# A hybrid encoder block on one core: the softmax of attention in a stage of its own, behind the next slot's turned queries

## The chip, the cores and the metric

The kernel runs on one core of a Trainium2 chip. The metric is the device time of one execution in microseconds (us); several executions are timed and their median is compared. One further execution is recorded by the profiler, and all rows below come from it.

## The reference, cut to what matters

One encoder block on a sequence of 1024 tokens with 1024 features, in float32. Two branches read the same normalised and projected input: gated linear attention, and windowed attention with grouped queries (8 query heads, 2 key and value heads of 128 features, blocks of 128 queries that see three blocks of 128 keys). The branches are merged, and a gated feed-forward layer follows. The change touches the windowed attention alone:

```python
q = _rope(_rms_norm(q...), pos); k = _rope(_rms_norm(k...), pos)
...
scores = jnp.einsum("bnqhgd,bnkhd->bnhgqk", qb, kc) * (hd ** -0.5)
scores = jnp.where(mask[None, :, None, None], scores, -jnp.inf)
sink = sinks.astype(f32).reshape(1, 1, hkv, grp, 1, 1)
m = jnp.maximum(scores.max(axis=-1, keepdims=True), sink)
p = jnp.exp(scores - m)
denom = p.sum(axis=-1, keepdims=True) + jnp.exp(sink - m)
o = jnp.einsum("bnhgqk,bnkhd->bnqhgd", p / denom, vc)
```

## The kernel before

Every float32 matrix product is made of three passes on TensorE (the engine PE): each operand is split into a high and a low part (`wh` and `wl`, `xh` and `xl`, `sqh` and `sql`, `ph` and `pl`), and high times high, low times high and high times low are summed in PSUM. The high part is a copy on ScalarE (ACT), the low part a subtraction on VectorE (DVE). So each operand costs one instruction on either engine.

The stage of windowed attention runs from about 390 to 570 us. Its work is cut into 16 units, one for each pair of a query block t and a key head g (four query heads each). A unit passes through a pipeline of six slots of the loop over `todo`; its steps and lines are:

- `prep` (L690 to 716, once for a block): load the projected queries and the next block's keys and values, squares (L696, L702), their sums (L704, on DVE), inverse roots, `rope_k`.
- `a_rope` (L725 to 728): the rotary products on DVE (L674, L676, L677).
- `a_turn` (L730 to 740): TensorE transposes the four heads of queries; ACT copies them out as `sqh` (L737), DVE makes `sql` (L738). `k_turn` does the same for keys (L721, L722).
- `a_scores`, four calls, one a head (L742 to 772): three score passes (L73), then a DVE instruction that adds the band mask and takes the row maximum (L752, the row-max). The last call also does the softmax of all four heads: on DVE the scaled maximum `mx` (L759), its bound by the sink `nm` (L760), `es` (L762); on ACT the exponentials (L763 for the sink, L766 four times, which also sum the row); on DVE the denominator `dn` (L768) and its reciprocal `rd` (L770); on ACT the normalising multiplication (L772, four times).
- `a_probs`, three calls, one a key block (L774 to 788): transposes of the probabilities, `ph` (L786) and `pl` (L787).
- `a_out` (L790 to 800): nine passes into one output, a copy `st` (L797) and its stores.

Unit n turns its queries in slot n+2, makes its scores in slot n+3, its probabilities' transposes in slot n+4 and its output in slot n+5. In one slot the steps of different units stand in the order `prep, a_rope, a_scores, a_turn, k_turn, a_out, a_probs`. So the softmax of a unit, written in the fourth call of `a_scores`, stands ahead of the turn of the following unit. Between two steps `slot` calls `fill`, which issues matrix products of the dense projections of the same input (L73 and L246 with the tile `mm`): TensorE has these while a step waits for the other engines.

TensorE's order is written out by hand (`tc.manual_schedule(engines={PE})`). The order on ACT, DVE and the DMA queue of SyncE (SP) comes from a scheduler that takes the program's order as its priority and places an instruction when it reckons its operands ready; `with tc.issue_after(x)` adds the one condition that what is written inside stands behind x on its engine. PSUM has four banks for dense products (`mm`) and four for the rest (`ch`). A new `ch` tile takes the bank that comes free first in the scheduler's order, and TensorE waits for the last reader of that bank.

Of the kernel before, what the change touches and what calls it, by code (L numbers as in the profile page):

```python
# [11 lines left out]
AF = mybir.ActivationFunctionType  # L12
# [12 lines left out]
SF = ((2, 50), (9, 24), (18, 18), (1 << 30, 12))  # L25
# [5 lines left out]
def body(tc, i, out):  # L31
    nc = tc.nc
    with ExitStack() as root:
# [8 lines left out]
        def nm(s):  # L42
            uid[0] += 1
            return f"{s}_{uid[0]}"
# [4 lines left out]
        def chtile(shape, dt=F32):  # L49
            return psc.tile(list(shape), dt, tag="ch", name=nm("ch"))  # L50
# [24 lines left out]
        def mm3(o, ah, al, bh, bl, start, stop):  # L75
            mm(o, ah, bh, start, False)
            mm(o, ah, bl, False, False)
            mm(o, al, bh, False, stop)
# [179 lines left out]
        def fill(n):  # L258

            while n > 0 and dense:  # L260
                try:
                    next(dense[0])
                    n -= 1
                except StopIteration:
                    dense.pop(0)

        def share(plan, t):
            return next(n for end, n in plan if t < end)
# [5 lines left out]
        def slot(stages, n):  # L274

            stages = [f for f in stages if f]
            done = 0
            if not stages:
                fill(n)
            for j, f in enumerate(stages):  # L280
                f()
                t = n * (j + 1) // len(stages)
                fill(t - done)
                done = t
# [340 lines left out]
        with tc.manual_schedule(engines={mybir.EngineType.PE}):  # L625
            fill(36)
            for t in range(last + 1):
                work = [[at[t, j]] for j in (0, 5, 4, 3, 2, 1) if (t, j) in at]
                if t in behind:
                    work = work or [[]]  # L630
# [38 lines left out]
        keys, att = {}, {}  # L669
# [60 lines left out]
        def a_turn(g, n):  # L730
            a = att[g, n]
            qt = chtile((P, 4, P))
            for h in range(4):
                nc.tensor.transpose(qt[:, h], a.qn[:, h], ident)
            a.qh = sw.tile([P, 4, P], FR, tag="qh", name=nm("sqh"))
            a.ql = sw.tile([P, 4, P], FR, tag="ql", name=nm("sql"))
            nc.scalar.activation(a.qh, qt, AF.Copy)  # L737
            nc.vector.tensor_tensor(a.ql, qt, a.qh.bitcast(F32), op=ALU.subtract)  # L738
            a.b0, a.b1 = max(n - 1, 0), min(n + 1, KT - 1)
            a.w = (a.b1 - a.b0 + 1) * P  # L740

        def a_scores(g, n, h):  # L742
            a = att[g, n]
            if h == 0:
                a.p = sw.tile([P, 4, 384], F32, tag="p", name=nm("p"))
                a.mx = sw.tile([P, 4], F32, tag="mx", name=nm("mx"))
            w, p, mx = a.w, a.p, a.mx
            ks = slice(a.b0 * P, (a.b1 + 1) * P)
            mo = (a.b0 - (n - 1)) * P
            s = chtile((P, 384))  # L750
            mm3(s[:, :w], a.qh[:, h], a.ql[:, h], kTh[:, g, ks], kTl[:, g, ks], True, True)
            nc.vector.tensor_tensor_reduce(out=p[:, h, :w], in0=s[:, :w], in1=band[:, mo:mo + w],  # L752
                                           op0=ALU.add, op1=ALU.max, scale=1.0, scalar=-1e30,
                                           accum_out=mx[:, h:h + 1])
            if h < 3:
                return
            sk = sink[:, 4 * g:4 * g + 4]
            nm_ = sw.tile([P, 4], F32, tag="nm", name=nm("nm"))
            nc.vector.scalar_tensor_tensor(mx, mx, -1.0, a.rs, op0=ALU.mult, op1=ALU.mult)  # L759
            nc.vector.tensor_tensor(nm_, mx, nsink[:, 4 * g:4 * g + 4], op=ALU.min)  # L760
            es = sw.tile([P, 4], F32, tag="es", name=nm("es"))
            nc.vector.tensor_tensor(es, sk, nm_, op=ALU.add)  # L762
            nc.scalar.activation(es, es, AF.Exp)  # L763
            dn = sw.tile([P, 4], F32, tag="dn", name=nm("dn"))
            for h in range(4):
                nc.scalar.activation(p[:, h, :w], p[:, h, :w], AF.Exp, bias=nm_[:, h:h + 1],  # L766
                                     scale=a.rs[:, h:h + 1], accum_out=dn[:, h:h + 1])
            nc.vector.tensor_tensor(dn, dn, es, op=ALU.add)  # L768
            rd = sw.tile([P, 4], F32, tag="rd", name=nm("rd"))
            nc.vector.reciprocal(rd, dn)  # L770
            for h in range(4):
                nc.scalar.activation(p[:, h, :w], p[:, h, :w], AF.Copy, scale=rd[:, h:h + 1])  # L772
# [40 lines left out]
        def xpart(q, k):  # L813
            r = xn.tile([P, HT], F32, tag="xn", name=nm("xn"))
            nc.sync.dma_start(out=r, in_=scr[f"x{q}", k])
            pool, th, tl, d = homes[q]
            XT[q].append(xsplit(pool, th.format(k + d), tl.format(k + d), r))
# [4 lines left out]
        for n in range(2 * KT):  # L822
            t, g = divmod(n, 2)
            todo[n + 5].append((a_out, g, t))
            todo[n + 4] += [(a_probs, g, t, kb) for kb in range(3)]
            todo[n + 3] += [(a_scores, g, t, h) for h in range(4)]
            todo[n + 2].append((a_turn, g, t))
            todo[n + 1].append((a_rope, g, t))
            if g == 0:
                todo[n + 1].append((prep, t))  # L830
                if t + 1 < KT:
                    todo[n + 2].append((k_turn, t + 1))
        order = (prep, a_rope, a_scores, a_turn, k_turn, a_out, a_probs)
        with tc.manual_schedule(engines={mybir.EngineType.PE}):
            for t, v in enumerate(todo):
                v.sort(key=lambda e: order.index(e[0]))
                if t > 2 * KT + 2 and v:
                    fill(8)
                slot([lambda e=e: e[0](*e[1:]) for e in v], share(SF, t))
                if t >= 2 * KT + 2:  # L840
                    assert len(dense) == 1
                    for q in ("T1", "22"):
                        xpart(q, t - 2 * KT - 2)
# [81 lines left out]
        def pair_T3(f):  # L925
            nme, m, a, b = PAIRS[f]
            g = pend[f]
            product(g.X, wsplit(g.s3, 512), XT["T3"], 4, False, True)
            return result((f"{nme}{m + 4}", 1), g.X, g.p5)
# [69 lines left out]
        with tc.manual_schedule(engines={mybir.EngineType.PE}):  # L999
# [15 lines left out]
            for j in range(0, len(PAIRS), 2):  # L1015
# [4 lines left out]
                v = [pair_T3(f) for f in two]  # L1020
# [53 lines left out]
        def gate(nme, s):  # L1074
            g = bt.tile([P, HT], F32, tag=nme[:2], name=nm(nme[:2]))
            nc.sync.dma_start(out=g, in_=scr[nme, s])
            nc.scalar.activation(g, g, AF.Sigmoid)
            return g
# [119 lines left out]
        with tc.manual_schedule(engines={mybir.EngineType.PE}):  # L1198
# [29 lines left out]
            for m in (0, 4, 1, 5, 2, 6, 3, 7):  # L1228
                g = [gate(f"gb{m}", s) for s in range(2)]
# [352 lines left out]
```

## Time and profile before

| | |
|---|---|
| median of 3 runs | 1625.35 us (1625.33 to 1625.67) |
| the profiled execution | 1624.31 us, span of its instructions 1622.5 us |
| TensorE (PE) busy | 1611.6 us, 99% |
| VectorE (DVE) busy | 1223.9 us, 75% |
| ScalarE (ACT) busy | 915.0 us, 56% |
| granted TensorE clock | 1.00 |

A row of the list of instructions has the start (us from the span's start), the length, the engine, the line, the operation, output and inputs by name, and shapes; in brackets stands how long the engine was idle just ahead of it and what ended that. Matmuls are pipelined, so the distance from one start to the next is what a matmul costs and its length is more than that.

### The profile page before, as it was taken

How to read it: one execution, taken by the hardware profiler on the slowest of the kernel's cores; microseconds unless marked ns; L12 is line 12 of the kernel's file. 1: busy time of each engine (PE TensorE's matmuls, PEld its weight loads, DVE VectorE, ACT ScalarE, POOL GpSimd, SP SyncE). 2: the span in 40 equal slices, each digit the busy share in tenths (PEclk: the TensorE clock that was granted, in tenths of full speed). 3: DMA queues.
4: the chain of work that ended last, by engine and by line, in shares of the span. 5: the costliest groups of instructions: out<-in, count | busy, mean ns of one | idle time of the engine just before them, and what ended most of it. 6: DMA issues, size and time to landing. Idle time of an engine off the chain costs nothing.

```text
span 1622.5 us, 23392 instructions
## 1 busy us (share of the span) xinstructions
PE 1611.6 (99%) x7644; PEld 1341.5 (83%) x7644; DVE 1223.9 (75%) x2315; ACT 915.0 (56%) x1883; POOL 0.2 (0%) x4
## 2 busy tenths in 40 slices
PE   9999999999999999999999999999999999999999
PEld 7888888888888888888888888888888888888887
DVE  8568888845999777876855878677777888789655
ACT  7456777873999745445732547754444444354442
POOL 0000000000000000000000000000000000000000
PEclk9999999999999999999999999999999999999999
DMA  8855757878554487878842656643435564695433
GB/s 279 295 180 194 252 172 256 274 264 284 176 162 143 129 268 253 270 242 263 282 126 89 192 192 214 196 141 124 136 121 177 170 219 146 207 328 189 149 98 117
DMA packets 196362, 323.25 MB, mean 199 GB/s; under 512 B 22318, under 2 KB 47790, under 8 KB 196240
## 3 DMA queue, kind: packets, MB, share of 16 engines
q1 hardware_dynamic: 196240, 321.76, 60.8%
q8 instruction: 60, 0.98, 0.2%
q14 instruction: 62, 0.51, 0.1%
HBM read 216.29 MB, written 105.38 MB: 198 GB/s over the span
## 4 chain that ended last, share of the span: by engine, by line
PE 89%; DVE 4%; ACT 3%; DMA 2%; issue 1%; SPq 0%; DVEq 0%; ACTq 0%
PE mm L73 20%; PE mm L877 10%; PE mm L879 10%; PE mm L878 10%; PE mm L1421 7%; PE ch L73 7%; PE ch L1421 6%; PE ch L878 5%; PE ch L879 5%; PE ch L877 5%; PE mm L246 3%; PE ch L783 1%; DMA kvr<-skv 1%; DMA st<-in_xT_dram 1%; DVE wl L69 0%
## 5 line engine op out<-in xcount | busy, mean ns | idle before, releaser
L856 ACT ACTIVATE wh<-ws 128x512 fp32r<-128x512 f32 x164 | 102.9, 629 | 152.5 <-PE mm L878 81.0
L73 PE MATMUL mm<-wh,xh 128*128 128x512 f32 x320 | 127.1, 397 | 0.0
L73 PE MATMUL mm<-wh,xl 128*128 128x512 f32 x320 | 127.1, 397 | 0.0
L73 PE MATMUL mm<-wl,xh 128*128 128x512 f32 x320 | 126.6, 395 | 0.0
L857 DVE TENSOR_TENSOR wl<-ws,wh 128x512 fp32r<-128x512 f32 x164 | 112.2, 686 | 14.0 <-ACT wh L856 13.5
L67 ACT ACTIVATE wh<-wr 128x512 fp32r<-128x512 f32 x118 | 73.5, 627 | 53.0 <-PE mm L73 21.3
L69 DVE TENSOR_TENSOR wl<-wr,wh 128x512 fp32r<-128x512 f32 x118 | 80.8, 686 | 25.2 <-ACT wh L67 22.8
L856 ACT ACTIVATE wh<-a 128x512 fp32r<-128x512 f32 x66 | 41.6, 632 | 89.1 <-PE ch L1421 42.3
L856 ACT ACTIVATE wh<-wr 128x512 fp32r<-128x512 f32 x76 | 47.8, 631 | 58.1 <-PE mm L878 17.6
L857 DVE TENSOR_TENSOR wl<-a,wh 128x512 fp32r<-128x512 f32 x66 | 45.5, 690 | 39.7 <-ACT wh L856 39.3
L1421 PE MATMUL mm<-hh,wl 128*128 128x512 f32 x176 | 68.6, 390 | 0.0
L1421 PE MATMUL mm<-hl,wh 128*128 128x512 f32 x176 | 68.5, 389 | 0.0
L1421 PE MATMUL mm<-hh,wh 128*128 128x512 f32 x176 | 68.5, 389 | 0.0
L73 PEld LDWEIGHTS mm<-wl,xh 128*128 128x128 f32 x320 | 60.2, 188 | 9.8
L73 PEld LDWEIGHTS mm<-wh,xl 128*128 128x128 f32 x320 | 60.2, 188 | 9.6
L73 PEld LDWEIGHTS mm<-wh,xh 128*128 128x128 f32 x320 | 60.3, 188 | 9.1 <-DVE st L141 0.2
L857 DVE TENSOR_TENSOR wl<-wr,wh 128x512 fp32r<-128x512 f32 x76 | 52.0, 685 | 7.8 <-ACT wh L856 7.1
L870 DVE TENSOR_TENSOR ws<-wr,wr 128x512 f32<-128x512 f32 x80 | 54.5, 687 | 4.3 <-DMA wr<-in_w_f_dram 1.7
L1388 DVE TENSOR_TENSOR hl<-hr,hh 128x512 fp32r<-128x512 f32 x77 | 52.8, 686 | 5.7 <-ACT hh L1387 5.4
L1387 ACT ACTIVATE hh<-hr 128x512 fp32r<-128x512 f32 x77 | 47.7, 619 | 9.0 <-DMA hr<-B 5.1
L1421 PE MATMUL ch<-hh,wh 128*128 128x512 f32 x132 | 51.3, 389 | 0.0
L1421 PE MATMUL ch<-hl,wh 128*128 128x512 f32 x132 | 51.3, 389 | 0.0
(454 smaller groups left out, 4984.5 us busy)
## 6 DMA issues: line engine op xcount, KB each, us to landing
wr<-in_w_fi_dram SPq DMA_DIRECT2D x110, 256.0 KB, 3.9
wr<-in_w_f_dram SPq DMA_DIRECT2D x100, 256.0 KB, 3.7
wh<-wh SPq DMA_DIRECT2D x80, 256.0 KB, 3.1
wl<-wl SPq DMA_DIRECT2D x80, 256.0 KB, 3.1
B<-c SPq DMA_DIRECT2D x44, 256.0 KB, 2.1
T<-st SPq DMA_DIRECT2D x44, 256.0 KB, 2.9
a<-in_w_fo_dram SPq DMA_DIRECT2D x44, 256.0 KB, 5.3
hr<-T SPq DMA_DIRECT2D x44, 256.0 KB, 2.7
```

What stands on the lines that cost most here:

```text
L67: nc.scalar.activation(h, raw, AF.Copy)
L69: nc.vector.tensor_tensor(l, raw, h.bitcast(F32), op=ALU.subtract)
L73: nc.tensor.matmul(o, a, b, start=start, stop=stop)
L246: nc.tensor.matmul(Y[q], w[:, c], x, start=f0, stop=f1, skip_group_check=True)
L856: nc.scalar.activation(h, src, AF.Copy)
L857: nc.vector.tensor_tensor(l, src, h.bitcast(F32), op=ALU.subtract)
L870: nc.vector.tensor_tensor(t, x, y, op=op)
L877: nc.tensor.matmul(o, h[:, c], x[kk][0], start=start and kk == 0, stop=False, skip_group_check=True)
L878: nc.tensor.matmul(o, h[:, c], x[kk][1], start=False, stop=False, skip_group_check=True)
L879: nc.tensor.matmul(o, l[:, c], x[kk][0], start=False, stop=kk == nk - 1, skip_group_check=True)
L1388: nc.vector.tensor_tensor(l, r, h.bitcast(F32), op=ALU.subtract)
L1421: nc.tensor.matmul(ys[m], a[:, c], b, start=f0, stop=f1, skip_group_check=True)
```

## The change

The softmax part of `a_scores` becomes a function `a_exps`, called by `a_soft`. In a slot that also turns the next unit's queries it is called right behind that `a_turn`, and everything in it is placed under `issue_after` of the `sqh` copy, so that ACT's exponentials stand behind this copy; in the last slots, which turn none, it is called behind the last `a_scores`, without the condition. From L753 on, line numbers grow by 8: L759 becomes L767, L760 L768, L766 L774, L772 L780, L786 and L787 L794 and L795, L797 L805; behind the stage they grow by 15.

```diff
-            nc.scalar.activation(a.qh, qt, AF.Copy)
+            turned.append(nc.scalar.activation(a.qh, qt, AF.Copy))
             nc.vector.tensor_tensor(a.ql, qt, a.qh.bitcast(F32), op=ALU.subtract)
...
                                            accum_out=mx[:, h:h + 1])
-            if h < 3:
-                return
+
+        turned = []
+
+        def a_soft(g, n, pin):
+            a = att[g, n]
+            w, p, mx = a.w, a.p, a.mx
+            with tc.issue_after(turned[-1].ins) if pin else nullcontext():
+                a_exps(a, g, w, p, mx)
+
+        def a_exps(a, g, w, p, mx):
             sk = sink[:, 4 * g:4 * g + 4]
...
-                slot([lambda e=e: e[0](*e[1:]) for e in v], share(SF, t))
+                work = [[e] for e in v]
+                names = [e[0] for e in v]
+                if a_scores in names:
+                    pin = a_turn in names
+                    k = names.index(a_turn) if pin else max(j for j, f in enumerate(names) if f is a_scores)
+                    g = v[names.index(a_scores)]
+                    work[k].append((a_soft, g[1], g[2], pin))
+                slot([lambda u=u: [f(*a) for f, *a in u] for u in work], share(SF, t))
```

What this does to the engines' order: TensorE's is the same. The numbers behind names in the rows below tell tiles of one kind apart; the rows have line, operation, output and inputs.

On ScalarE, in the slot in which unit 1 has its scores, before:

```order
L766 ACTIVATE p_5539,dn_5574<-p_5539,nm_5568,rs_5237 128x256
L763 ACTIVATE es_5571<-es_5571 128x4
L766 ACTIVATE p_5539,dn_5574<-p_5539,nm_5568,rs_5237 128x256 x3
L737 ACTIVATE sqh_5594<-ch_5589 128x512
L721 ACTIVATE kTh<-ch_5600 128x2x128
L772 ACTIVATE p_5539<-p_5539,rd_5580 128x256 x4
L786 ACTIVATE ph_5612<-ch_5607 128x512
L786 ACTIVATE ph_5624<-ch_5619 128x512
```

And now:

```order
L737 ACTIVATE sqh_5576<-ch_5571 128x512
L771 ACTIVATE es_5583<-es_5583 128x4
L774 ACTIVATE p_5539,dn_5586<-p_5539,nm_5580,rs_5237 128x256 x4
L721 ACTIVATE kTh<-ch_5600 128x2x128
L794 ACTIVATE ph_5612<-ch_5607 128x512
L780 ACTIVATE p_5539<-p_5539,rd_5592 128x256 x4
L794 ACTIVATE ph_5624<-ch_5619 128x512
```

The exponentials moved behind the copy `sqh`. This is the one slot in which they stood ahead of it before; in the others they stood behind it already.

On ScalarE in the slot around 520 us, before:

```order
L766 ACTIVATE p_6989,dn_7032<-p_6989,nm_7026,rs_6545 128x384
L763 ACTIVATE es_7029<-es_7029 128x4
L766 ACTIVATE p_6989,dn_7032<-p_6989,nm_7026,rs_6545 128x384 x3
L797 COPY st_7073<-ch_7063 128x512
L786 ACTIVATE ph_7086<-ch_7081 128x512
L786 ACTIVATE ph_7096<-ch_7091 128x512
L772 ACTIVATE p_6989<-p_6989,rd_7038 128x384 x4
L786 ACTIVATE ph_7107<-ch_7102 128x512
```

And now:

```order
L805 COPY st_7073<-ch_7063 128x512
L774 ACTIVATE p_6989,dn_7043<-p_6989,nm_7037,rs_6545 128x384
L771 ACTIVATE es_7040<-es_7040 128x4
L774 ACTIVATE p_6989,dn_7043<-p_6989,nm_7037,rs_6545 128x384 x3
L794 ACTIVATE ph_7086<-ch_7081 128x512
L794 ACTIVATE ph_7096<-ch_7091 128x512
L794 ACTIVATE ph_7107<-ch_7102 128x512
L780 ACTIVATE p_6989<-p_6989,rd_7049 128x384 x4
```

The copy of a finished output moved ahead of the exponentials, and the third `ph` ahead of the normalising multiplications.

On VectorE around 440 us, ahead of the first row-max of a unit, before:

```order
L676 TENSOR_TENSOR qn_6258<-kvr_6245,kA 128x256
L770 RECIPROCAL rd_5829<-dn_5823 128x4
L674 TENSOR_TENSOR rq_6094<-qr_5922,qB 128x4x64 x2
L787 TENSOR_TENSOR pl_5881<-ch_5875,ph_5880 128x512
L676 TENSOR_TENSOR qr_5922<-qr_5922,qA 128x512
L752 ISA p_5958,mx_5959<-ch_5960,band 128x384
```

And now:

```order
L674 TENSOR_TENSOR rq_6094<-qr_5922,qB 128x4x64
L795 TENSOR_TENSOR pl_5881<-ch_5875,ph_5880 128x512
L676 TENSOR_TENSOR qr_5922<-qr_5922,qA 128x512
L676 TENSOR_TENSOR qn_6258<-kvr_6245,kA 128x256
L677 TENSOR_TENSOR qr_5922<-qr_5922,rq_6094 128x512
L752 ISA p_5958,mx_5959<-ch_5960,band 128x384
```

The key product `qn` (L676) and the query sum `qr` (L677) moved ahead of the row-max. Of the banks, unit by unit, most stay; near 534 us the second head's score tile takes the bank of the first head's and the third's that of the second's, and so does one pair near 544 us.

## The prediction

> **What bounds the kernel now.** I read the page first, then stretches of 20 us through the attention stage, then the list of instructions around each place where TensorE pauses there.
>
> ```profile
> span 1622.5 us, 23392 instructions
> PE 1611.6 (99%) x7644; PEld 1341.5 (83%) x7644; DVE 1223.9 (75%) x2315; ACT 915.0 (56%) x1883; POOL 0.2 (0%) x4
> ```
>
> TensorE (PE) is busy for 1611.6 of 1622.5 us, so all waits of the program together are worth 10.9 us. The change adds and removes no matmul and leaves their order alone. It can move the end only through TensorE's waits between 390 and 570 us, where attention runs (columns: stretch, length, busy time and count of PE, its weight loads, DVE, ACT, POOL, then clock, DMA share, GB/s):
>
> ```profile
> 390.00:570.00 180.00, 178.13 (x953) 149.84 (x952) 152.93 (x438) 153.56 (x374) 0.00 (x0) 1.00 0.51 162
> 420.00:440.00 20.00, 19.76 (x106) 16.62 (x105) 19.76 (x61) 18.16 (x48) 0.00 (x0) 1.00 0.44 132
> 480.00:500.00 20.00, 20.00 (x110) 17.22 (x109) 19.29 (x56) 18.43 (x46) 0.00 (x0) 1.00 0.43 133
> 520.00:540.00 20.00, 20.00 (x111) 17.28 (x110) 19.18 (x55) 16.84 (x40) 0.00 (x0) 1.00 0.45 134
> ```
>
> Two things are to be seen. TensorE idles for 1.87 us of the 180, so little can be won. And VectorE (19.2 to 19.8 of 20 us) and ScalarE (16.8 to 18.4) are nearly full, so what is put ahead of an urgent instruction there delays it by its whole length; only slack on TensorE's side absorbs it.
>
> **What can be won.** The largest pause before 500 us that the new order touches is at 421.71:
>
> ```profile
> 419.01 1.48 DVE L704 TENSOR_REDUCE ss<-sq 128x10 f32<-128x1280 f32 x1
> 420.40 0.68 DVE L676 TENSOR_TENSOR qr<-qr,qA 128x512 f32<-128x512 f32 x1
> 421.00 0.55 DVE L752 CUSTOM_DVE_ANT_0 p<-ch,band 128x384 f32<-128x384 f32 x1
> 421.07 0.40 PE L73 MATMUL mm<-wl,xh 128*128 128x512 f32 x1
> 421.71 0.47 PE L73 MATMUL ch<-ph,vSh 128*128 128x512 f32 x1 [0.24 <-ACT sqh L737]
> ```
>
> A dense pass is followed by the next start after 0.23, as at 449.60 to 449.83 below; here 0.64 pass, so 0.41 is lost, and some 0.1 more in the start that follows a pause, as at 450.70 below. The profile names the sqh copy, but the PSUM bank that this output takes was last read by the row-max of 421.00, which stands behind the 1.48 reduction L704 and the rope product L676. In the new order that row-max stands ahead of both: -0.5. The idle column shows 0.24 for this 0.5, so the 1.87 of the window stands for about twice that, 3.8 us, from start to start; this is the ceiling of any gain.
>
> **What the change moves.** By the written-out order ScalarE's exponentials stood already behind the next slot's sqh copy in every slot but n=1; so the pin itself moves one slot's. The rest follows: the scheduler, given another program order, shuffles VectorE and ScalarE within the stage, and the banks of the "ch" pool go out in another sequence. No instruction is added on TensorE, POOL stays, SP exchanges a few neighbouring loads and stores, which I cost at nothing: the xn and wr loads are read by splits that stand in dense work, and DMA is at 0.43 to 0.51. If that cover went, an L807 split would be late by one load. I price the places where something lands ahead of work that TensorE soon waits for.
>
> At 440 the key rope's L676 and the query's L677 now precede the row-max that frees the bank of a head:
>
> ```profile
> 436.88 0.42 DVE L676 TENSOR_TENSOR qn<-kvr,kA 128x256 f32<-128x256 f32 x1
> 439.15 0.55 DVE L752 CUSTOM_DVE_ANT_0 p<-ch,band 128x384 f32<-128x384 f32 x1
> 440.04 0.34 PE L73 MATMUL ch<-kTh,sqh 128*128 128x384 f32 x1
> 442.43 0.69 DVE L677 TENSOR_TENSOR qr<-qr,rq 128x512 f32<-128x512 f32 x1
> ```
>
> Added ahead: 0.42 and 0.69, together 1.11 (about 1.0 as they overlap their neighbours); the row-max ended at 439.70, so 0.34 is slack. Between 0, if L676 and L677 fall into a wait for transposed queries or keys, and 0.71; I take the middle, +0.35.
>
> At 493 the split sql and the rope product now stand ahead of nm, the exponentials' bias:
>
> ```profile
> 487.72 0.69 DVE L738 TENSOR_TENSOR sql<-ch,sqh 128x512 fp32r<-128x512 f32 x1
> 488.39 0.42 DVE L674 TENSOR_TENSOR rq<-qr,qB 128x256 f32<-128x256 f32 x1
> 488.73 0.69 DVE L69 TENSOR_TENSOR wl<-wr,wh 128x512 fp32r<-128x512 f32 x1
> 492.01 0.69 DVE L787 TENSOR_TENSOR pl<-ch,ph 128x512 fp32r<-128x512 f32 x1
> 493.17 0.33 PE L73 MATMUL ch<-kTh,sqh 128*128 128x384 f32 x1
> ```
>
> nm comes 1.0 later (487.72 to 488.73, the start of what stood behind the two), and with it the exponentials, the transposes and pl. pl is read out at 492.70, 0.47 ahead of the score at 493.17 that takes its bank: 0, if the dense work between absorbs it, to 0.53; +0.3, a little over the middle, because both engines are full here.
>
> At 514 the last split of a probability block already frees its bank too late, and a rope product and an xl split are put ahead of it:
>
> ```profile
> 512.47 0.68 DVE L807 TENSOR_TENSOR xl<-xn,xh 128x512 fp32r<-128x512 f32 x1
> 513.16 0.40 DVE L674 TENSOR_TENSOR rq<-qr,qB 128x256 f32<-128x256 f32 x1
> 513.47 1.28 DVE L787 TENSOR_TENSOR pl<-ch,ph 128x512 fp32r<-128x512 f32 x2
> 514.21 0.44 PE L73 MATMUL ch<-kTh,sqh 128*128 128x384 f32 x1
> ```
>
> No slack (the first pl ends near 514.1), and 0.68 more ahead: 0 to 0.68. As pl also waits for ph, some of the 0.68 falls into that wait: +0.3.
>
> At 525 a copy of attention output (L797) moves ahead of the exponentials:
>
> ```profile
> 519.98 0.71 ACT L766 ACTIVATE p<-p,nm,rs 128x384 f32<-128x384 f32 x1 [0.20 <-DVE nm L760]
> 520.24 0.39 PE L73 MATMUL ch<-ph,vSl 128*128 128x512 f32 x1
> 522.86 0.56 ACT L797 COPY st<-ch 128x512 f32<-128x512 f32 x1
> 523.33 1.07 ACT L786 ACTIVATE ph<-ch 128x512 fp32r<-128x512 f32 x2
> 524.00 1.26 DVE L787 TENSOR_TENSOR pl<-ch,ph 128x512 fp32r<-128x512 f32 x2
> 524.85 0.37 PE L73 MATMUL ch<-kTh,sqh 128*128 128x384 f32 x1
> ```
>
> The copy reads what the matmul of 520.24 finishes at 520.63, so the exponentials start at 520.63+0.56=1.2 us later than 519.98; 0.47 comes back where the copy stood. So ph starts 0.7 later, the first pl ends 0.7 later, and the score at 524.85, which has next to no slack (0.24 after its predecessor), waits: 0 to 0.75, +0.6 taken, near the upper end for want of slack.
>
> At 534 to 536 the second head's scores now go into the first head's bank and the third's into the second's; a head's next start must then wait for the row-max of the head just before. Such a pair stands in the trace:
>
> ```profile
> 449.43 0.34 PE L73 MATMUL ch<-kTh,sql 128*128 128x384 f32 x1
> 449.60 0.39 PE L246 MATMUL mm<-xl,wh 128*128 128x512 f32 x1
> 449.80 0.56 DVE L752 CUSTOM_DVE_ANT_0 p<-ch,band 128x384 f32<-128x384 f32 x1
> 449.83 0.40 PE L246 MATMUL mm<-xh,wl 128*128 128x512 f32 x1
> 450.42 0.45 PE L73 MATMUL ch<-kTh,sqh 128*128 128x384 f32 x1 [0.19 <-DVE mx L752]
> 450.70 0.34 PE L73 MATMUL ch<-kTl,sqh 128*128 128x384 f32 x1
> 534.75 0.33 PE L73 MATMUL ch<-kTh,sqh 128*128 128x384 f32 x1
> ```
>
> From 449.83 to 450.42 are 0.59 instead of 0.23, and from 450.42 to 450.70 0.28 instead of the 0.18 between score passes: 0.36+0.10=0.46. Two pairs without other cover: +0.9 (0.5, if later banks come free, to 0.95).
>
> At 544.56 the same happens to a pair, where a bank wait stands already:
>
> ```profile
> 544.21 0.40 PE L246 MATMUL mm<-xh,wh 128*128 128x512 f32 x1
> 544.56 0.36 PE L73 MATMUL ch<-kTh,sqh 128*128 128x256 f32 x1
> 562.91 0.50 PE L73 MATMUL ch<-ph,vSh 128*128 128x512 f32 x1 [0.51 <-ACT ph L786]
> ```
>
> There 0.35-0.23=0.12 is replaced by 0.46: +0.3. The wait at 562.91 ends the last slot, has a chain of its own and stays.
>
> **The sum.** -0.5+0.35+0.3+0.3+0.6+0.9+0.3=+2.25, say +2.3 us. The profiled execution took 1624.31 with its span of 1622.5; the median of the runs is 1.04 above it. The difference goes on the median: 1625.35+2.3=1627.65, say 1627.6, +0.14%. A difference under 0.2% (3.25 us) is about what a measurement of this kernel can't tell from none.
>
> [...]
>
> **The rivals.**
> Slower beyond 0.2%: nm comes later in six slots, by the instructions put ahead of it 0.60, 0.94, 0.34, 0.34, 0.90 and 0.60 (starts of sql, wl and rq to the next start, as 487.72 to 488.39 to 488.73), sum 3.72. The full VectorE and ScalarE speak for it: then exponentials, normalise, transposes and the output's matmuls wait in each slot. Against it: between nm and the first use of the probabilities TensorE has dense work in every slot, and 480 to 500 shows no idle at all. Passed on in full, with -0.5 and the two bank terms of 534 and 544 (1.2): 3.72+1.2-0.5=+4.4, about 1629.8. It decides if more than 2.5 of the 3.72 are passed on. Chance 0.28.
>
> Faster or no slower: the added waits fall into slack and only removals count: -0.5 at least, up to half of the ceiling, -1.9; about 1624.4. For it: every unknown above has 0 as its lower end but the bank pairs. Chance 0.12; beyond 0.2% it needs 3.25 of the 3.8, 0.03 at most.
>
> The change does little: since ScalarE had its order already, all terms are within the scheduler's guess and cancel: 1625.35±0.5. Chance 0.15.
>
> Clock: the windows show 1.00 throughout, though TensorE paused for 0.2 to 0.5. [...] Nothing in this trace shows a lower clock. Chance 0.02. [...]
>
> **How the numbers follow.** My forecast, bank and order terms partly paid, +1 to +3.2: chance 0.43. With the rivals (0.28, 0.12, 0.15, 0.02) that is 1. The likeliest gives 1627.6; its own range is 1626.3 to 1628.6. The range for 8 in 10 leaves out half of the faster case beyond -0.75 and a part of the slow one above +5.2: 1624.6 to 1630.6. Slower by over 0.2%: 0.28 and 0.02, 0.30. Faster by over 0.2%: 0.03. The same: 0.67.
>
> **What would show it.** TensorE's start at 421.7 without its 0.41 pause; a pause of 0.3 to 0.5 before the second and third head near 534 to 536, released by mx; the copy L805 ahead of the exponentials near 520 and a pause before the score at 525; clock 1.00. Wrong would be the forecast if the busy time lost by TensorE between 390 and 570 us is unchanged or smaller, or if pauses appear behind late nm in the slots from 450 to 530 that I cost at little.

## The result, and the profile after

The changed kernel takes 1628.38 us (median of 14 runs, 1626.58 to 1630.54) against 1624.03 us (14 runs, 1622.91 to 1625.67): the ratio is 1.0024 with a 95% interval of 1.0016 to 1.0032. It is slower by 2.6 to 5.2 us, just about the 0.2% that the prediction took for the limit of measuring. The head of the page of after:

```profile
span 1626.5 us, 23390 instructions
PE 1614.2 (99%) x7644; PEld 1342.1 (83%) x7644; DVE 1223.8 (75%) x2315; ACT 915.5 (56%) x1883; POOL 0.2 (0%) x4
```

VectorE and ScalarE did the same work for the same time (1223.8 and 915.5 us); only TensorE's waits grew. The stretch from 385 to 580 us, before and after (third column: PE busy):

```profile
385.00:580.00 195.00, 193.13 (x1020) 162.19 (x1019) 161.91 (x457) 159.00 (x386) 0.00 (x0) 1.00 0.53 171
```

```profile
385.00:580.00 195.00, 190.71 (x1000) 158.09 (x999) 161.01 (x455) 157.91 (x384) 0.00 (x0) 1.00 0.52 164
```

TensorE idles for 4.29 us in place of 1.87, and has 20 matmuls fewer done at the end of the stretch. As its order is the same in both kernels, each matmul's start can be set against its start before. From 385 to 580 us the difference grows by 4.47 us; this number is called the stage's loss from here on, and is given for each run against the one profile of before. TensorE's idle time grew by 2.42 for it: a pause stands in the profile for about half of what it costs from start to start, as the prediction assumed. The difference grows in steps, at the places of these rows of after (all PE; in brackets idle time and what ended it):

```profile
421.98 0.39 PE L73 MATMUL mm<-wl,xh 128*128 128x512 f32 x1
422.21 0.40 PE L73 MATMUL ch<-ph,vSh 128*128 128x512 f32 x1
440.83 0.44 PE L73 MATMUL ch<-kTh,sqh 128*128 128x384 f32 x1 [0.22 <-DVE mx L752]
494.65 0.44 PE L73 MATMUL ch<-kTh,sqh 128*128 128x384 f32 x1 [0.25 <-DVE pl L795]
515.88 0.44 PE L73 MATMUL ch<-kTh,sqh 128*128 128x384 f32 x1 [0.38 <-DVE pl L795]
527.40 0.42 PE L73 MATMUL ch<-kTh,sqh 128*128 128x384 f32 x1 [0.72 <-DVE pl L795]
537.96 0.44 PE L73 MATMUL ch<-kTh,sqh 128*128 128x384 f32 x1 [0.20 <-DVE mx L752]
539.41 0.44 PE L73 MATMUL ch<-kTh,sqh 128*128 128x384 f32 x1 [0.20 <-DVE mx L752]
549.14 0.38 PE L73 MATMUL ch<-kTh,sqh 128*128 128x256 f32 x1
567.84 0.51 PE L73 MATMUL ch<-ph,vSh 128*128 128x512 f32 x1 [0.84 <-ACT ph L794]
```

At 422.21 there is no pause any more (0.23 after its predecessor); everywhere else one is new or longer. The steps, with the start that follows each pause, beside the prediction's terms:

| place (before) | predicted us | measured us |
|---|---|---|
| 407 and 416 | none | +0.14, +0.30 |
| 421.7 | -0.5 | -0.48 |
| 440 | +0.35 | +0.48 |
| 472 | none | +0.07 |
| 492 to 493 | +0.3 | +0.19 and +0.52 |
| 514 | +0.3 | +0.19 (+0.26 at the start that waits, -0.07 at the head before) |
| 525 | +0.6 | +0.89 |
| 534 to 537, second and third head | +0.9 | +0.46 and +0.47 |
| the same, first and fourth head | none | +0.26 and +0.28 |
| 544 | +0.3 | +0.41 one head earlier, +0.10 at its own place |
| 562.9 | 0 | +0.33 |

They sum to 4.6; two starts that came 0.07 to 0.08 earlier make it 4.47. Outside the stage the two profiles differ at two places, where the runs of the series differ among each other too: after is 0.45 later when the stage begins (it comes at 152 us), and at 942 us it waits 0.9 less. With these, 0.45+4.47-0.9 makes the 4.0 by which the two spans differ.

### The profile page after: what moved, and what is told of

Read it like the earlier page. It is cut to its first block, busy times and chain, and to the rows that moved or that the text cites. A ratio compares the mean times of both kernels' runs of the same rounds, so it can differ in the third digit from the quotient of the medians.

```text
span 1626.5 us, 23390 instructions
## 1 busy us (share of the span) xinstructions
PE 1614.2 (99%) x7644; PEld 1342.1 (83%) x7644; DVE 1223.8 (75%) x2315; ACT 915.5 (56%) x1883; POOL 0.2 (0%) x4
## 4 chain that ended last, share of the span: by engine, by line
PE 83%; DVE 7%; ACT 6%; DMA 2%; issue 1%; SPq 0%; ACTq 0%; DVEq 0%
PE mm L73 16%; PE mm L894 10%; PE mm L892 10%; PE mm L893 10%; PE mm L1436 7%; PE ch L1436 6%; PE ch L894 5%; PE ch L892 5%; PE ch L893 5%; PE ch L73 5%; PE mm L246 3%; ACT p L774 1%; DVE G L422 1%; DVE wl L69 1%; DMA kvr<-skv 1%
```

## The experiments

Stage's loss in all runs, in us against before: changed kernel 4.47, e1 2.37, e2 -0.09, e3 -0.27, e4 1.42, e5 4.61, e6 2.81, e7 2.63, e8 7.26, e9 0.37, e10 -1.79, e11 -1.33. Each is read from one profile. Runs of one order differ by 0.2 at 421 and by up to 0.8 at 407 and 417, where loads come at other times, as this row of e5 shows (the keys' load held VectorE for 0.54):

```profile
415.75 0.49 DVE L674 TENSOR_TENSOR sq<-kvr,kB 128x128 f32<-128x128 f32 x2 [0.54 <-DMA kvr<-skv]
```

**Without the condition.**

```diff
-                    pin = a_turn in names
...
-                    work[k].append((a_soft, g[1], g[2], pin))
+                    behind = a_turn in names and u in range(16)
...
+                    work[k].append((a_soft, g[1], g[2], behind and u in ()))
```

The last argument, which asks for the condition, is never true here, as no u is in the empty `()`.

> The softmax is written behind the turn as in the changed kernel, but without the condition that queues it behind the copy of the turned queries. Theory (the place in the program does it: written later, the softmax gets a lower priority, ScalarE and VectorE take other work first, and TensorE pauses for copies and splits that end late): +3 to +5.5 us against the kernel before, with the pauses near 494, 516, 527 and 537 to 541 us still there. Rival (the condition does it): 0 +- 0.7 us, and none of these pauses.

Measured: 1626.97 against 1624.39 us, ratio 1.0017 (1.0007 to 1.0026). The pauses at 494, 516 and at the second and third head near 536 are there; that at 527 is not. So the place in the program costs by itself, but 2.4 of the 4.5 us, less than the theory's 3; the condition is not innocent either.

**The condition where it binds.** Only unit 1 has the softmax behind the turn, and behind the copy.

```diff
-                    pin = a_turn in names
-                    k = names.index(a_turn) if pin else max(...)
...
-                    work[k].append((a_soft, g[1], g[2], pin))
+                    u = 2 * g[2] + g[1]
+                    behind = a_turn in names and u in (1,)
+                    k = names.index(a_turn) if behind else max(...)
+                    work[k].append((a_soft, g[1], g[2], behind and u in (1,)))
```

> Only unit 1 has its softmax behind the turn and behind the copy: the one unit whose exponentials the condition really moves on ScalarE. Every other unit as before. Theory: -0.5 us at 421.7, +0.1 at 407, up to +0.3 at 416, nothing behind 480 us: 0 +- 0.7 us in all. Rival (the condition does it, as it binds here alone): +3 us or more.

Measured: 1623.79 against 1624.39 us, ratio 0.9997 (0.9988 to 1.0007). The -0.48 at 421.7 came, +0.30 at 416 too, and a pause that no one had listed, 0.90 at 436; the pauses of before at 452, 472 and 513 to 514 went, though nothing was changed there. That is the scheduler's ripple: one moved unit, at 412 us, turns orders on VectorE up to 523 us. So the theory held in its sum, not place by place, and the condition alone is not what costs.

**Halves.** The same edit, with units 0 to 7 and with units 8 to 15 in place of unit 1.

> Units 0 to 7 have the softmax behind the turn, 8 to 15 as before. Theory of independent local pauses: the changed kernel's own differences up to 494 us and none behind, +1.2 us (+0.42 up to 417, -0.48 at 421.7, +0.48 at 440.8, +0.07 at 473, +0.19 and +0.50 at 493 and 494). Rival (each late unit makes the next one later, so that the start decides): the pauses at 516, 527 and 537 to 548 come too, +3.5 us or more.

> Units 8 to 15 have the softmax behind the turn, 0 to 7 as before. On VectorE the splits sql and the rope products stand ahead of nm in the late slots as in the changed kernel; on ScalarE the copies of the output and the normalising multiplications keep their old places, and of the banks only the pair at 544 us is another. Theory of independent local pauses: the rest of the 4.5 us, +3.3 us, from 514 us on. Rival 1 (ScalarE's order and the banks near 534 do it, and a nm that VectorE makes later costs nothing): only the pair at 544 to 549, +0.3 to +0.6 us. Rival 2 (the later nm does it): +1.5 to +2.5 us with pauses before the second head in several slots.

Measured: units 0 to 7 1624.81 (ratio 1.0002, 0.9993 to 1.0012), units 8 to 15 1625.43 (1.0007, 0.9997 to 1.0016) against 1624.39 us. The stage's loss is -0.27 and 1.42: together 1.15, where both halves at once give 4.47. Of the 1.42, 0.42 stand at 450, where e4 still has the order of before and VectorE waited 1.10 for the keys' load. So the pauses don't add, and the theory of independent pauses fell, as did the rival that the early units decide. In neither half does ScalarE's order near 520 and 534 turn; it turns only with both. What in the scheduler's reckoning tips it was not traced and stays open.

Of the two rivals of e4, the late nm is the nearer: its pauses came, though their sum is less than its +1.5. With ScalarE's two slots in their old order, e4 loses 0.36 at 493, 0.33 at the heads near 534, 0.13 at 544 and 0.33 at 562.9, and gains 0.3 from 512 to 525. These rows of it show the late keys at 450, then the exponentials late for nm, ph ahead of the multiplications, and the second head's pause:

```profile
450.76 0.49 DVE L674 TENSOR_TENSOR sq<-kvr,kB 128x128 f32<-128x128 f32 x2 [1.10 <-DMA kvr<-skv]
531.78 0.71 ACT L774 ACTIVATE p<-p,nm,rs 128x384 f32<-128x384 f32 x1 [1.36 <-DVE nm L768]
535.13 1.07 ACT L794 ACTIVATE ph<-ch 128x512 fp32r<-128x512 f32 x2
536.49 0.44 PE L73 MATMUL ch<-kTh,sqh 128*128 128x384 f32 x1
```

**The two orders that turned, put back one by one.** In the slot near 520 the copy L805 stands ahead of the exponentials. Of after, ScalarE and VectorE:

```profile
521.75 0.15 DVE L768 TENSOR_TENSOR nm<-mx,nsink 128x4 f32<-128x4 f32 x1
522.34 0.59 ACT L805 COPY st<-ch 128x512 f32<-128x512 f32 x1 [0.93 <-PE ch L73]
522.82 0.71 ACT L774 ACTIVATE p<-p,nm,rs 128x384 f32<-128x384 f32 x1
525.69 1.53 ACT L794 ACTIVATE ph<-ch 128x512 fp32r<-128x512 f32 x3
```

nm is ready at 521.90, but ScalarE waits 0.93 for the output's last matmul, copies it, and starts the exponentials at 522.82. In the slot near 534 the normalising multiplications stand ahead of ph; after, and then before:

```profile
533.02 0.71 ACT L774 ACTIVATE p<-p,nm,rs 128x384 f32<-128x384 f32 x1 [1.50 <-DVE nm L768]
536.49 2.13 ACT L780 ACTIVATE p<-p,rd 128x384 f32<-128x384 f32 x4
538.53 1.54 ACT L794 ACTIVATE ph<-ch 128x512 fp32r<-128x512 f32 x3
539.88 1.88 DVE L795 TENSOR_TENSOR pl<-ch,ph 128x512 fp32r<-128x512 f32 x3
```

```profile
529.35 0.71 ACT L766 ACTIVATE p<-p,nm,rs 128x384 f32<-128x384 f32 x1 [0.43 <-DVE nm L760]
532.70 1.07 ACT L786 ACTIVATE ph<-ch 128x512 fp32r<-128x512 f32 x2
533.66 2.13 ACT L772 ACTIVATE p<-p,rd 128x384 f32<-128x384 f32 x4
```

The exponentials waited 1.50 for nm in place of 0.43, and the four multiplications (2.13) now stand between them and ph, so the first pl ends at 540.5, three microseconds behind the second head's turn.

```diff
-            nc.scalar.copy(ob, o)
+            with tc.issue_after(exped[-1].ins) if 2 * n + g + 2 in (11,) else nullcontext():
+                nc.scalar.copy(ob, o)
```

Here `exped` lists the last exponential of each unit.

> The changed kernel with one more condition: the copy of a finished output near 520 us (L805, unit 9) is queued on ScalarE behind the exponentials of unit 11, where it stood before. Theory (this copy waits for TensorE's output and holds the exponentials behind it): the pause of 0.89+0.08 us at 527.4 goes, and the stage ends 1.0 us earlier than in the changed kernel; the pauses at 537 to 541 stay, since the normalising multiplications there keep their place. Rival (nm is late anyway, so the exponentials can't start earlier): 0 to -0.2 us, the pause at 527.4 stays.

Measured: 1628.03 against 1624.13 us, ratio 1.0024 (1.0014 to 1.0034). The exponentials now start with nm, and the pause shrinks from 0.89 to 0.26:

```profile
522.25 0.71 ACT L774 ACTIVATE p<-p,nm,rs 128x384 f32<-128x384 f32 x1 [0.53 <-DVE nm L768]
525.13 0.56 ACT L807 COPY st<-ch 128x512 f32<-128x512 f32 x1
...
526.59 0.40 PE L246 MATMUL mm<-xh,wl 128*128 128x512 f32 x1
527.08 0.41 PE L73 MATMUL ch<-kTh,sqh 128*128 128x384 f32 x1
```

So the copy was 0.63 of it. Where the other 0.26 come from stays open: ScalarE waits 0.53 for nm here, in place of 0.20 before, but e2, which has nm and the exponentials at this place as before, pauses as long:

```profile
519.66 0.71 ACT L774 ACTIVATE p<-p,nm,rs 128x384 f32<-128x384 f32 x1 [0.20 <-DVE nm L768]
524.33 0.40 PE L246 MATMUL mm<-xh,wl 128*128 128x512 f32 x1
524.85 0.41 PE L73 MATMUL ch<-kTh,sqh 128*128 128x384 f32 x1
```

The score starts 0.52 behind its predecessor, where before took 0.24. The time does not show the gain, as this profile of e5 has 0.77 more at 417.

```diff
+            if u not in (12,):
+                a_norm(a)
...
+                    if 2 * g[2] + g[1] in (12,):
+                        k = [j for j, f in enumerate(names) if f is a_probs][1]
+                        work[k].append((late_norm, g[1], g[2]))
...
+        def late_norm(g, n):
+            with tc.issue_after(split[-1].ins):
+                a_norm(att[g, n])
```

Here `a_norm` holds the four multiplications, and `split` lists the copies ph.

> The changed kernel with unit 12's four normalising multiplications queued on ScalarE behind the first two splits ph of unit 11, where they stood before. The banks of the heads near 534 to 541 us are then those of before too. Theory (late ph and pl hold the banks; that heads follow each other in one bank is only how the scheduler gets round it): the pauses of 0.46, 0.47 and 0.28 us at 538.0, 539.4 and 540.7 go, -1.2 us against the changed kernel; the pause at 527.4 stays. Rival (they come from late scores, not from the multiplications): pauses of the same sum at the first use of the banks that pl frees.

Measured: 1626.92 against 1624.13 us, ratio 1.0017 (1.0007 to 1.0027); the stage loses 1.66 less than the changed kernel. Of that, 1.0 stands at the heads near 537, 0.40 at 548 and 0.25 at 407 and 416, where runs of one order differ too; so the edit itself gave 1.4, for 1.2 expected. The heads near 537:

```profile
535.23 1.07 ACT L800 ACTIVATE ph<-ch 128x512 fp32r<-128x512 f32 x2
536.20 2.13 ACT L786 ACTIVATE p<-p,rd 128x384 f32<-128x384 f32 x4
...
536.60 0.44 PE L73 MATMUL ch<-kTh,sqh 128*128 128x384 f32 x1
537.69 0.34 PE L73 MATMUL ch<-kTh,sqh 128*128 128x384 f32 x1
```

The third head starts 1.09 behind the second, where the changed kernel took 1.45; of the second's pause 0.12 is left. The banks near 534 are those of before again, so this run alone doesn't part order from banks; e8 does.

> Both conditions of the two runs before. Theory (two separate causes): -2.2 us against the changed kernel, +2.2 us against the kernel before. Rival (both are one lag that is only passed on): not more than the larger of the two alone, -1.2 us.

Measured, with both edits: 1626.46 against 1624.13 us, ratio 1.0013 (1.0004 to 1.0023). At their own places both gains are there (-0.63 at 527, -1.0 from 537 to 541, -0.38 at 548), -2.0 in sum; the two are separate causes. The stage shows 1.84 of it, because this run lost 0.2 more at 407 and 416 together.

**The banks put back, the order left.** The four banks of the "ch" pool get a tag each, and a table says which tile takes which; the table is that of the changed kernel but for the four heads and the turn near 534.

```diff
+CH = (...)
...
-            return psc.tile(list(shape), dt, tag="ch", name=nm("ch"))
+            k = next(ch_at)
+            return psc.tile(list(shape), dt, tag=f"ch{CH[k]}", name=nm("ch"), bufs=1)
```

> The changed kernel with its banks of the ch pool written out as a table, and in it the four heads near 534 to 541 us and the turn behind them given the banks that they had before; ScalarE's order in the stage is that of the changed kernel but for one small exponential near 553 us. Theory of the prediction (heads that follow each other in one bank cause the pauses): the pauses at 538.0 and 539.4 go, -0.9 us against the changed kernel. Rival (the late splits cause them and the bank is only where it shows): the second head must wait for the pl that ends at 540.56, a pause of 2.5 to 3.1 us in place of 0.46+0.47+0.28, +1.3 to +2 us.

Measured: 1632.28 against 1624.13 us, ratio 1.0049 (1.0032 to 1.0065), with only three runs, from 1629.77 to 1633.11. TensorE's rows, and the same place in windows of 1 us (clock in the third column from the end):

```profile
539.68 0.41 PE L80 MATMUL ch<-kTh,sqh 128*128 128x384 f32 x1 [2.21 <-DVE pl L802]
...
541.38 0.63 PE L253 MATMUL mm<-xl,wh 128*128 128x512 f32 x1
541.80 0.63 PE L253 MATMUL mm<-xh,wl 128*128 128x512 f32 x1
```

```profile
540.00:541.00 1.00, 1.00 (x7) 0.91 (x6) 1.00 (x3) 0.30 (x1) 0.00 (x0) 1.00 0.00 0
541.00:542.00 1.00, 1.00 (x5) 0.91 (x4) 1.00 (x4) 0.00 (x0) 0.00 (x0) 0.54 0.03 8
542.00:543.00 1.00, 1.00 (x5) 0.91 (x4) 0.27 (x2) 0.00 (x0) 0.00 (x0) 0.50 0.38 141
543.00:544.00 1.00, 1.00 (x4) 0.75 (x3) 0.57 (x3) 0.00 (x0) 0.00 (x0) 0.50 0.35 125
544.00:545.00 1.00, 1.00 (x7) 0.91 (x6) 0.67 (x2) 0.10 (x1) 0.00 (x0) 0.75 0.04 12
```

With the banks of before the second head waits 2.37 (2.21 idle) for the late pl in place of 0.36. The stage loses 2.8 more than in the changed kernel, in two parts: 1.2 is the longer wait, as the rival said (+1.3 to +2), and 1.55 are the starts from 541 to 544.5, where the clock was halved. Heads that follow each other in one bank were the cheaper way round a late pl, not the cause.

**The bias in its old place.** Three instructions of VectorE, 128x4 elements each, go back behind the fourth head's scores; all else of the change stays. The function `a_bias` holds them, mx, nm and es, taken out of `a_exps`.

```diff
+            if h == 3:
+                a_bias(a, g)
```

> The changed kernel with three instructions of VectorE, the scaled maximum mx, its bound nm and es, written again behind the fourth head's scores; the exponentials and all that follows stay behind the turn and behind the copy, in every slot. The rows of every engine then stand as in the run with unit 1 alone. Theory (the loss comes from nm, which in the new place loses its turn on VectorE to sql and the rope products, not from queueing the exponentials): the stage takes as long as before, -0.1 +- 0.3 us, the time within 0.1% of the kernel before. Rival (the place of the exponentials does it): +2.5 us or more, as in the run without the condition.

Measured: 1624.76 against 1624.26 us, ratio 1.0002 (0.9993 to 1.0011). The order on all engines is that of e2, instruction by instruction. The stage loses 0.37, which is 0.46 more than in e2, and at 407 alone the two differ by 0.53. At 493, from 534 to 544 and at 562.9 it loses nothing. ScalarE's wait for nm, in the list of waits from 385 to 580 us (total us, times, longest), after and in this run:

```profile
ACT p L774 <- DVE nm L768: 8.7, 10, 2.1
```

```profile
ACT p L771 <- DVE nm L784: 5.8, 8, 2.1
```

In before it was 7.2 us. The total does not measure the loss: e4 waits 8.9 and loses 1.42, e1 waits 5.3 and loses 2.37. What decides is that three instructions went back and the loss went from 4.47 to 0.37. So it was the place of nm and its two neighbours on VectorE that set the loss off, in the main; the three were not moved one by one. With them in their old place the queueing of the exponentials costs nothing that the runs show.

**A pause that the change has nothing to do with.**

```diff
-                    fill(8)
+                    fill(14 if t == 2 * KT + 3 else 8)
```

> The kernel before with 14 dense passes ahead of the output of unit 14 instead of 8 (fill in the slot at 561 us); the six come from the dense work further behind. Theory (TensorE has nothing to do at 562.9 while ph and pl of this unit are made, 0.66+0.49+0.11 us): the pauses go, -1.2 us against the kernel before. Rival (the six passes are missed behind, where the next stage's first work waits): 0.

Measured: 1622.28 against 1624.26 us, ratio 0.9988 (0.9979 to 0.9997).

```profile
385.00:580.00 195.00, 194.34 (x1028) 163.83 (x1027) 162.57 (x455) 159.34 (x385) 0.00 (x0) 1.00 0.55 173
...
562.18 0.39 PE L246 MATMUL mm<-xh,wh 128*128 128x512 f32 x1
562.41 0.39 PE L73 MATMUL ch<-ph,vSh 128*128 128x512 f32 x1
```

The pauses are gone, and TensorE is busy 1.21 us more in the stage. At this place the starts come 1.3 earlier, as the theory said; the other 0.5 of the stage's -1.79 stand at 407 and 421, which the edit does not touch. By its interval this version beats both kernels, the one before by 0.5 to 3.4 us.

> Units 0 to 7 with the softmax behind the turn, the others as before, and the 14 dense passes at 561 us. If both gains add: -0.3 and -1.2, -1.5 us against the kernel before, the fastest of all. If the tail's passes are missed behind: -0.3 us.

Measured: 1623.18 against 1624.26 us, ratio 0.9992 (0.9983 to 1.0001): the tail's pause is gone here too, but a further gain from units 0 to 7 does not show.

## Why the prediction was right, and where it was not

The direction, the stage, the mechanism (TensorE's pauses behind late readers of PSUM) and the range held. The likeliest value was +2.3 us, measured are +4.35 by the medians and +4.47 in the stage, beyond the likeliest case's own upper end of +3.2 and in the part above 0.2% that was given 0.30. That the time itself, 1628.38, lies inside that case's 1626.3 to 1628.6 is luck: it was counted from 1625.35, the median of three runs, and the kernel before took 1624.03 in 14. By its steps:

- **421.7:** -0.5 against -0.48. Shown, also in e2 and e3.
- **440, 514:** +0.35 and +0.3 against +0.48 and +0.19; a middle between bounds was a fair choice, but neither cause was tested alone, and the pause of 514 went in e2, e3 and e4 by ripple.
- **493:** mis-sized, +0.3 against 0.71. The first score's own bank wait for the copy (0.19) was left out, and pl came 0.4 later than its slack.
- **525:** +0.6 against 0.89. e5 shows 0.63 for the copy, as priced; the rest stays open, since e2 has it without a later nm.
- **534 to 537:** the price of a pair was right to the hundredth (0.46 and 0.47 for 0.46), its cause was not. The prediction blamed the banks, so the match is luck. e8 put the banks back and lost 1.2 more before any drop of the clock; e6 put ScalarE's order back and 1.0 of the 1.2 at these three heads went. The row to read was the order of the normalising multiplications against ph, which it did not price.
- **544 and 562.9:** 0.3 against 0.51, and "stays" against +0.33. The pair's own place shows 0.10; the 0.41 stands one head earlier and went in e6, so it belongs to the late ph too. The last wait has a chain of its own, but its chain is made of the same exponentials; it is in e4 and not in e9, so it comes with the later nm.
- **407, 416:** +0.44 that the sum had no term for; runs of one order differ by as much there.
- **The pin "moves one slot's":** true of the order (e2), but it was taken for harmless. Without it the changed kernel loses 2.4, with it 4.5; with nm early it costs nothing (e9).
- **The rival of the late nm** gave +4.4, nearly the time measured, and named the right origin, but not the way. nm was not passed on by its 3.72 slot by slot: the later place turned the order of ScalarE's instructions in two slots, which cost 2.0, and e4 shows 1.15 that go with a later nm at 493, 534, 544 and 562.9 with these orders unturned. The prediction's own sign against it, pauses behind a late nm from 450 to 530 that it cost at little, came in part, with 0.71 for 0.3 at 493.
- **The clock:** 1.00 in the profile of after, with pauses up to 0.9 in the stage, so that rival, with its 0.02, fell there. No run shows that pauses of this length lower the clock; e8 shows it at 0.50 once, behind an idle time of 2.21 us, and the starts there lost 1.55.

Of the 4.5 us, e9 shows the origin and e5 to e7 the way for 2.0; the rest, at 440, 493, the heads near 534 and in the tail, is partly in e4, but no experiment took it apart one by one.

## What to carry to other kernels

Where a scheduler takes program order as priority, moving a long stage moves its small instructions as well: here three of 128x4 elements in each unit, not the long exponentials, cost about 4 us in all. Move what must wait and leave the short instruction that releases it where it was (e9: a loss of 0.37 in place of 4.47). A bank that is reused at once is a sign to look for the reader that ends late elsewhere (here the first pl, which ended at 540.5 in after); and before shuffling a tuned stage, look whether its last pause has dense work left to put into it (e10: the starts there come 1.3 earlier).

## What the runs showed of the hardware that was not expected

In e8 TensorE's clock was halved behind one idle time of 2.21 us: it went on at 1.00 for about 1.4 us behind the pause, then stood at 0.54, 0.50 and 0.50 for three windows of 1 us and at 0.75 in the fourth, with dense passes 0.42 apart in place of 0.23. Shorter idle times did not do that in the profiles of before and after: 1.08 near 292.6 and 1.10 near 293.1, each ended by ob (L522), with the clock at 1.00 in both throughout. Neither did 1.50 in e8 itself, behind which the next passes stand 0.31 and 0.23 apart:

```profile
951.10 0.47 PE L899 MATMUL mm<-S6h,wh 128*128 128x512 f32 x1 [1.50 <-DVE st L1186]
951.41 0.39 PE L900 MATMUL mm<-S6l,wh 128*128 128x512 f32 x1
951.64 0.40 PE L901 MATMUL mm<-S6h,wl 128*128 128x512 f32 x1
```

The drop near 541 takes 0.46+0.50+0.50+0.25=1.71 us of full clock, and the mean clock of this execution, 0.999 of 1631.2 us, has room for one of that size, not for two. The three executions of e8 have a mean clock of 0.999, 0.998 and 1.000; what the drop depends on, no run shows.
